# Hybrid encoder step: chunk 1's operands behind the residual, chunk 2 first in the last products, and products without a reader at both ends

## The chip, the cores and the metric

The kernel runs on one core of a Trainium2 chip. The metric is the device time of one execution in microseconds (us). The median of three runs before is 1571.35 us (1571.05 to 1572.93). A profiled execution, recorded apart, gives the span, the busy times and the timeline that the text reads. Its times count from the first instruction of the span.

The engines are named as in the profile: PE (TensorE, matrix products; PEld its weight loads), DVE (VectorE), ACT (ScalarE), POOL (GpSimd) and SP (SyncE, which issues nearly all DMAs here). Each works through its own queue in order and waits for the others on semaphores.

## The reference, cut to what matters

One layer runs over 1152 rows (1024 of a prompt and 128 of eight short streams) with 1024 features. The change touches the end of the first sub-layer and the feed-forward part:

```python
def layer(x, ...):
    h = rmsnorm(x, p['g_pre1'])
    z = h @ p['w_in']
    ...
    x = x + rmsnorm(merged @ p['w_out'], p['g_post1'])
    h2 = rmsnorm(x, p['g_pre2'])
    f, conv_new = conv_ffn(h2, conv_buf, p['w_ffn_up'], p['w_dw'], p['b_dw'], p['w_ffn_down'])
    x = x + rmsnorm(f, p['g_post2'])

def conv_ffn(h, buf, w_ffn_up, w_dw, b_dw, w_ffn_down):
    up = h @ w_ffn_up
    a, g = jnp.split(up, 2, axis=-1)
    ...
    act = jax.nn.gelu(conv) * g
    return act @ w_ffn_down, ext[:, -(CONV_W - 1):]
```

`rmsnorm` divides each row by the root of its mean square and scales by a gain. `w_ffn_up` is 1024 x 5632, `w_ffn_down` 2816 x 1024.

## The kernel before, in words

Activations lie with features on the 128 partitions and rows along the free dimension. The 1152 rows are cut into three **chunks** c = 0, 1, 2 of 384 columns. Every f32 product is made of three products of split operands (`mm3`, lines 102 to 108): each operand has a hi part, written by ACT as a copy, and a lo part, which is the difference and is made on DVE or POOL (`split`, lines 61 to 65). So an operand costs ACT one copy and DVE one subtraction (L63, L64), and a tile of 8 feature blocks costs PE 24 products (L104, L107, L108).

A **row norm** goes through four engines: squares on ACT, sums over partitions as small products with a vector of ones on PE, `rsqrt` (L85 on ACT, L87 a power on POOL), three diagonal tiles on ACT (`row_bcast`, L95), and one f32 product on PE (L97) that spreads the row factors over all partitions into a PSUM bank. DVE then multiplies rows by it.

`start` makes the first products of chunk 0 as soon as the first features of x and the first weights have been loaded and split.

`phase_o` multiplies by `w_out`, chunk after chunk, then adds the residual (`resid`: L1103 scales by the row factors, L1107 adds x, squares L1058 and L1061 on ACT, their sums L1065 on DVE) and norms again (`norm`, L1125). Chunks 0 and 1 enter the up GEMM in Strassen-Winograd form: B11, B21 are the halves of chunk 0, B12, B22 the halves of chunk 1, and T1 to T4 are sums of them; all of these are operands to be split (`op`). While chunk 2's residual and norm are made, PE works on four tiles of the up GEMM for chunk 0 and four for chunk 1 (`plain`: s0 and s1 are the first two blocks of `w_ffn_up`, "a" and "g" its two halves). L1170, L1202 to L1204 make the T sums on DVE. Chunk 2 goes through the up GEMM plainly, from `h2hi` and `h2lo`.

`phase_u` runs the other 20 blocks, `phase_d` the down GEMM: seven products M1 to M7 for chunks 0 and 1 over four groups of features, plain products for chunk 2 into y2. The sums of the parts M make the result rows (L1633 to L1648). The last four feature blocks are added as whole products, `last_down`, in the order of chunks 0, 1, 2; PE holds eight PSUM banks in turn (four `ps`, four `pc`), and DVE adds each bank to its row (L1560). Between these, `final_rms` and `final_rows` norm the chunk before (L1598 scales, L1600 on DVE and L1601 on POOL add x2, SP stores y).

A scheduler orders the instructions of each engine by a simulated timeline; `high_priority`, `issue_after` and `keep_in_program_order` bind it where the code says so.

Of the kernel before, what the change touches and what calls it, by code (L numbers as in the profile page):

```python
# [32 lines left out]
class K:  # L33
# [27 lines left out]
    def split(self, hi, lo, src, eng=None):  # L61
        nc = self.nc
        a = nc.scalar.activation(hi, src, AF.Copy)  # L63
        (eng or nc.vector).tensor_sub(lo, src, hi)  # L64
        return a

# [191 lines left out]
    def start(self, P, pair, done, z):  # L258
        nc = self.nc
        self.hhi, self.hlo = [], []  # L260
        sh = (128, 4, 256)
        I = self.I
        x0 = self.h_load(0, (0,))
        halves = slice(0, 4), slice(4, 8)
        rw = [self.rawtile([128, 8, 128])]
# [765 lines left out]
    def phase_o(self):  # L1031
# [6 lines left out]
        if True:  # L1038
# [50 lines left out]
            def resid(c, rs):  # L1089
# [4 lines left out]
                for f in range(8):  # L1094
# [10 lines left out]
                    if f % 2:  # L1105
                        for k in range(2):
                            pin(V.tensor_add(oT[:, f - 1 + k, :], oT[:, f - 1 + k, :], x[:, k, :]))  # L1107
                    if f % 2:
# [33 lines left out]
            for c in range(3):  # L1142
                ss.append(ssa())
                for f in range(8):
# [7 lines left out]
                    if c:  # L1152
                        if f == 0:
                            rs = sums(ss[c - 1])
                        elif f == 1:
                            with tc.high_priority():
                                ss2 = resid(c - 1, rs)
                        elif f == NF[c]:
                            rs = sums(ss2)
                        elif f == NF[c] + 1:  # L1160
                            with tc.high_priority():
                                norm(c - 1, rs)
                            if c == 1:
                                op("B11", h0[:, lo])
                                op("B21", h0[:, up])
                                V.tensor_sub(h0[:, up], h0[:, up], h0[:, lo])
                            else:
                                op("B12", h1[:, lo])
                                op("B22", h1[:, up])
                                V.tensor_sub(h0[:, lo], h1[:, lo], h0[:, lo])  # L1170
                                op("T1", h0[:, lo])
            wms.close()
# [18 lines left out]
            with tc.high_priority():  # L1191
                ss2 = resid(2, rs)
            plain(s1, "a", 0)
            plain(s1, "g", 0)
# [6 lines left out]
            plain(s1, "g", 1)  # L1201
            V.tensor_sub(h1[:, lo], h1[:, up], h1[:, lo])  # L1202
            V.tensor_sub(h1[:, up], h1[:, up], h0[:, lo])
            V.tensor_sub(h0[:, up], h0[:, up], h1[:, lo])  # L1204
            with tc.issue_after(last.ins):
                op("T3", h1[:, lo])
# [152 lines left out]
    def phase_d(self):  # L1359
# [6 lines left out]
        with ExitStack() as ctx:  # L1366
# [188 lines left out]

            def last_down(last, c, f, acc):

# [8 lines left out]
                nc.scalar.activation(sq, y, AF.Square)  # L1566
                if c == 2 and f > 5:
                    acc.append(sq)
# [14 lines left out]

            def final_rows(c, rs):

# [4 lines left out]
                for f in range(0, 8, 2):  # L1590
                    if c == 1:
                        x2 = self.rawtile([128, 2, 384], "x2r")
# [7 lines left out]
                    order(V.tensor_add(y[0], y[0], x2[:, 0, :]))  # L1600
                    G.tensor_add(y[1], y[1], x2[:, 1, :])  # L1601
                    for k in range(2):
# [22 lines left out]
            for g in range(NW):  # L1625
# [5 lines left out]
                prod(cur, 2)  # L1631
                if last:
                    G.tensor_add(M[2], M[2], M[1])  # L1633
                for f in range(8):
# [3 lines left out]
                for p in (3, 4, 5, 6, 7):  # L1638
                    prod(cur, p)
                    if last and p == 6:  # L1640
                        V.tensor_add(M[6], M[6], M[1])
                        V.tensor_add(M[5], M[5], M[6])
                        G.tensor_add(M[4], M[4], M[6])
                        V.tensor_add(M[3], M[3], M[5])
                    if last and p == 7:
                        for f in range(4):
                            V.tensor_add(M[4][:, f], M[4][:, f], M[7][:, f])
                        G.tensor_add(M[5], M[5], M[7])  # L1648
                    next(nx, None)
# [3 lines left out]
            accs = Mt[3][:, 1].rearrange("p (c k) n -> p c k n", c=2)  # L1653
            acc = [[accs[:, c % 2, 0]] for c in range(3)]
            rows = iter(())
            for c in range(3):
                for f in range(8):
                    last_down(cur, c, f, acc[c])
                    if c:
                        if f == 1:  # L1660
                            rs = final_rms(acc[c - 1])
                        elif f == 3:
                            rows = final_rows(c - 1, rs)
                            next(rows)
                        elif f > 3:
                            next(rows, None)
                if c == 1:
                    for _ in rows:
                        pass
            with tc.issue_after(self.evac.ins):  # L1670
                rs = final_rms(acc[2])
                for _ in rows:
                    pass
            for _ in final_rows(2, rs):
                pass
# [178 lines left out]
```

## Time and profile before

| | |
|---|---|
| median of 3 runs | 1571.35 us |
| profiled execution, its own time | 1571.99 us |
| its span, first to last instruction | 1570.2 us |
| mean granted clock of PE | 0.991 |
| DMA moved | 161.34 MB, 103 GB/s |

The span is 1.8 us shorter than the execution's own time. Busy times are shares of that span. In a timeline row stand the start and the duration in us, engine, line, operation, output and inputs by the program's names, shapes, the count of merged instructions, and in brackets the idle time of the engine before it with what ended it. A duration of a product is longer than the distance to the next product, since products overlap; the pace is read from start to start. The page's row PEclk is the granted clock of PE in tenths.

### The profile page before, as it was taken

How to read it: one execution, taken by the hardware profiler on the slowest of the kernel's cores; microseconds unless marked ns; L12 is line 12 of the kernel's file. 1: busy time of each engine (PE TensorE's matmuls, PEld its weight loads, DVE VectorE, ACT ScalarE, POOL GpSimd, SP SyncE). 2: the span in 40 equal slices, each digit the busy share in tenths (PEclk: the TensorE clock that was granted, in tenths of full speed). 3: DMA queues.
4: the chain of work that ended last, by engine and by line, in shares of the span. 5: the costliest groups of instructions: out<-in, count | busy, mean ns of one | idle time of the engine just before them, and what ended most of it. 6: DMA issues, size and time to landing. Idle time of an engine off the chain costs nothing.

```text
span 1570.2 us, 22880 instructions
## 1 busy us (share of the span) xinstructions
PE 1535.1 (98%) x8988; PEld 1503.1 (96%) x8988; DVE 1018.3 (65%) x1606; ACT 583.3 (37%) x895; POOL 447.9 (29%) x427
## 2 busy tenths in 40 slices
PE   8999999999999999999899999999999999999996
PEld 7999998888999999999899999999999999999996
DVE  8956987656533364547576665665566569788866
ACT  8313444344311251444354333333333343333322
POOL 0000010000111234200215444344344301575446
PEclk9999999999999999999999999999999999999998
DMA  7533334432422234223213212112221234222315
GB/s 269 168 104 103 104 113 164 133 104 80 159 71 72 82 105 148 93 83 117 91 44 116 84 56 85 71 58 82 71 83 57 84 129 137 77 94 90 111 46 171
DMA packets 98028, 161.34 MB, mean 103 GB/s; under 512 B 23168, under 2 KB 68608, under 8 KB 97920
## 3 DMA queue, kind: packets, MB, share of 16 engines
q1 hardware_dynamic: 97488, 159.65, 30.9%
q8 instruction: 70, 1.15, 0.3%
q14 instruction: 38, 0.31, 0.1%
q10 hardware_dynamic: 432, 0.23, 0.1%
HBM read 117.43 MB, written 42.42 MB: 102 GB/s over the span
## 4 chain that ended last, share of the span: by engine, by line
PE 85%; DVE 7%; DMA 3%; issue 2%; ACT 1%; POOL 1%; SPq 0%; POOLq 0%; ACTq 0%; DVEq 0%
PE pc L108 16%; PE pc L107 16%; PE pc L104 16%; PE ps L104 11%; PE ps L107 11%; PE ps L108 11%; DMA Ts<-DG 1%; DMA DG<-gs 1%; PE ps L850 1%; POOL rs_y L87 1%; DVE mg L1125 0%; PE ps L97 0%; PE ps L764 0%; PE ps L816 0%; DVE Xs L599 0%
## 5 line engine op out<-in xcount | busy, mean ns | idle before, releaser
L104 PE MATMUL pc<-hhi,whi 128*128 128x384 f32 x760 | 258.0, 339 | 6.6 <-ACT hhi L127 6.6
L107 PE MATMUL pc<-hlo,whi 128*128 128x384 f32 x760 | 257.2, 338 | 0.1
L108 PE MATMUL pc<-hhi,wlo 128*128 128x384 f32 x760 | 256.7, 338 | 0.3 <-DVE wlo L64 0.3
L63 ACT ACTIVATE whi<-rawt 128x1024 fp32r<-128x1024 f32 (+1 forms) x99 | 103.5, 1047 | 189.0 <-PE pc L107 85.5
L64 DVE TENSOR_TENSOR wlo<-rawt,whi 128x1024 fp32r<-128x1024 f32 (+1 forms) x99 | 122.4, 1238 | 56.3 <-ACT whi L63 56.0
L104 PEld LDWEIGHTS pc<-hhi,whi 128*128 128x128 f32 x760 | 143.5, 189 | 9.1 <-ACT hhi L127 6.6
L107 PEld LDWEIGHTS pc<-hlo,whi 128*128 128x128 f32 x760 | 143.5, 189 | 2.3 <-issue 0.5
L108 PEld LDWEIGHTS pc<-hhi,wlo 128*128 128x128 f32 x760 | 143.4, 189 | 2.3 <-issue 0.7
L201 DVE TENSOR_TENSOR sg<-pc,rb 128x384 f32<-128x384 f32 x95 | 52.4, 554 | 115.5 <-PE pc L108 113.7
L108 PE MATMUL pc<-h2hi,wlo 128*128 128x384 f32 x352 | 118.9, 338 | 0.0
L107 PE MATMUL pc<-h2lo,whi 128*128 128x384 f32 x352 | 118.3, 336 | 0.5 <-DVE h2lo L64 0.5
L104 PE MATMUL pc<-h2hi,whi 128*128 128x384 f32 x352 | 118.3, 336 | 0.0
L63 ACT ACTIVATE S<-S 128x512 fp32r<-128x512 f32 x80 | 50.3, 629 | 149.2 <-PE ps L108 88.9
L64 DVE TENSOR_TENSOR S<-S,S 128x512 fp32r<-128x512 f32 x80 | 66.6, 835 | 49.7 <-ACT S L63 47.7
L925 ACT ACTIVATE sg<-sg,vec 128x384 f32<-128x384 f32 x72 | 44.1, 613 | 139.8 <-DVE sg L201 112.0
L104 PE MATMUL ps<-bT,S 128*128 128x384 f32 x240 | 80.2, 334 | 0.0
L107 PE MATMUL ps<-bT,S 128*128 128x384 f32 x240 | 80.2, 334 | 0.0
L108 PE MATMUL ps<-bT,S 128*128 128x384 f32 x240 | 80.2, 334 | 0.0
L1012 POOL TENSOR_TENSOR mg<-mg,sgl 128x384 f32<-128x384 f32 x24 | 29.1, 1213 | 165.6 <-DVE sgl L1010 162.2
L63 ACT ACTIVATE dhi<-dwr 128x1024 fp32r<-128x1024 f32 x38 | 39.6, 1058 | 83.2 <-PE pc L107 54.6
L87 POOL TENSOR_TENSOR rs_y<-rs_v,mhalf 128x3 f32<-128x3 f32 (+1 forms) x13 | 18.8, 1445 | 174.8 <-ACT rs_v L85 174.7
L107 PEld LDWEIGHTS pc<-h2lo,whi 128*128 128x128 f32 x352 | 66.0, 187 | 0.8 <-DVE h2lo L64 0.8
(446 smaller groups left out, 4277.8 us busy)
## 6 DMA issues: line engine op xcount, KB each, us to landing
rawt<-in_w_up SPq DMA_DIRECT2D x44, 512.0 KB, 3.4
Dact<-t SPq DMA_DIRECT2D x22, 576.0 KB, 3.6
rawt<-in_w_gate SPq DMA_DIRECT2D x24, 512.0 KB, 3.5
dwr<-in_w_down SPq DMA_DIRECT2D x22, 512.0 KB, 3.5
Dsg<-sg SPq DMA_DIRECT2D x45, 192.0 KB, 1.9
sgl<-Dsg SPq DMA_DIRECT2D x45, 192.0 KB, 2.4
dBr<-Dact SPq DMA_DIRECT2D x8, 768.0 KB, 5.1
xT<-in_xT SPq DMA_DIRECT2D x12, 384.0 KB, 7.2
```

The costliest lines, as they stand in the source:

```text
L63: a = nc.scalar.activation(hi, src, AF.Copy)
L64: (eng or nc.vector).tensor_sub(lo, src, hi)
L87: nc.gpsimd.tensor_tensor(y, v, self.mhalf[:, 0:n], op=OP.pow)
L104: i = nc.tensor.matmul(out, whi, xhi, start=start, stop=False)
L107: nc.tensor.matmul(out, whi, xlo, start=False, stop=False)
L108: nc.tensor.matmul(out, wlo, xhi, start=False, stop=stop)
L201: self.nc.vector.tensor_mul(sg, b, self.rb[:, c, :])
L850: nc.tensor.matmul(o, va[:, m, 2 * hp + e, :], pT[:, m, :], start=m == 0, stop=m == 1)
L925: self.nc.scalar.activation(sg, sg, AF.Sigmoid, bias=self.vec[:, V_BGATE + m:V_BGATE + m + 1])
L1012: nc.gpsimd.tensor_add(m, m, sp)
```

## The change

Four edits:

1. In `start`, a memset of the row-factor tile and eight f32 products of it with the ones tile are put ahead of the first product. Nothing reads their result.
2. In `phase_o`, the copies of B12 and B22 are issued after the diagonal tiles of chunk 2's residual, and the subtraction and copy for T1 after the residual's last add (`resid_last`). `split` returns both its instructions, so that the last two subtractions for T2 and T4 can be issued after the last lo part of h2.
3. In `phase_d`, the last products run over chunks 2, 0, 1. The sums of parts are written between chunk 2's last products, one of POOL's goes to DVE, and the rows of a normed chunk start one product tile earlier. The last add of the last chunk goes from POOL to DVE.
4. Ahead of the last row broadcast twelve products of the last operands are put into a free bank. Nothing reads their result.

```diff
@@ split
         a = nc.scalar.activation(hi, src, AF.Copy)
-        (eng or nc.vector).tensor_sub(lo, src, hi)
-        return a
+        return a, (eng or nc.vector).tensor_sub(lo, src, hi)
@@ start
         x0 = self.h_load(0, (0,))
+
+        rb = self.rb[:, 0]
+        nc.vector.memset(rb, 0.0)
+        b = self.sm()[:, 0:384]
+        for _ in range(8):
+            self.tc.keep_in_program_order(nc.tensor.matmul(b, self.ones, rb, start=True, stop=True))
@@ phase_o, resid
-                            pin(V.tensor_add(oT[:, f - 1 + k, :], oT[:, f - 1 + k, :], x[:, k, :]))
+                            self.resid_last = V.tensor_add(oT[:, f - 1 + k, :], oT[:, f - 1 + k, :], x[:, k, :])
+                            pin(self.resid_last)
@@ phase_o, after norm of chunk 1
-                            else:
-                                op("B12", h1[:, lo])
-                                op("B22", h1[:, up])
-                                V.tensor_sub(h0[:, lo], h1[:, lo], h0[:, lo])
-                                op("T1", h0[:, lo])
@@ phase_o, after plain(s0, "g", 0) and resid(2, rs)
+            with tc.issue_after(self.diag.ins):
+                op("B12", h1[:, lo])
+                op("B22", h1[:, up])
+            with tc.issue_after(self.resid_last.ins):
+                V.tensor_sub(h0[:, lo], h1[:, lo], h0[:, lo])
+                op("T1", h0[:, lo])
+                V.tensor_sub(h1[:, lo], h1[:, up], h1[:, lo])
@@ phase_o, end
-            V.tensor_sub(h1[:, lo], h1[:, up], h1[:, lo])
-            V.tensor_sub(h1[:, up], h1[:, up], h0[:, lo])
-            V.tensor_sub(h0[:, up], h0[:, up], h1[:, lo])
-            with tc.issue_after(last.ins):
+            with tc.issue_after(last[1].ins):
+                V.tensor_sub(h1[:, up], h1[:, up], h0[:, lo])
+                V.tensor_sub(h0[:, up], h0[:, up], h1[:, lo])
+            with tc.issue_after(last[0].ins):
@@ phase_d, last_down and final_rows
-                if c == 2 and f > 5:
+                if end and f > 5:
...
-                    if c == 1:
+                    if i == 2:
...
-                    G.tensor_add(y[1], y[1], x2[:, 1, :])
+                    (V if (i, f) == (3, 6) else G).tensor_add(y[1], y[1], x2[:, 1, :])
@@ phase_d, last group
-                if last:
-                    G.tensor_add(M[2], M[2], M[1])
...
-                    if last and p == 6:
-                        V.tensor_add(M[6], M[6], M[1])
-                        V.tensor_add(M[5], M[5], M[6])
-                        G.tensor_add(M[4], M[4], M[6])
-                        V.tensor_add(M[3], M[3], M[5])
-                    if last and p == 7:
-                        for f in range(4):
-                            V.tensor_add(M[4][:, f], M[4][:, f], M[7][:, f])
-                        G.tensor_add(M[5], M[5], M[7])
@@ phase_d, last products
+            sums = {(0, 0): ((G, 2, 1), (V, 6, 1)), (0, 1): ((V, 4, 6),), (0, 3): ((V, 4, 7),), (0, 4): ((V, 5, 6),),
+                    (0, 6): ((V, 3, 5),), (0, 7): ((G, 5, 7),)}
+            order = (2, 0, 1)
+            for i, c in enumerate(order):
                 for f in range(8):
-                    last_down(cur, c, f, acc[c])
-                    if c:
+                    last_down(cur, c, f, acc[i], i == 2)
+                    for e, p, q in sums.get((i, f), ()):
+                        e.tensor_add(M[p], M[p], M[q])
+                    if i:
                         if f == 1:
-                            rs = final_rms(acc[c - 1])
+                            rs = final_rms(acc[i - 1])
                         elif f == 3:
-                            rows = final_rows(c - 1, rs)
+                            rows = final_rows(order[i - 1], rs, i)
                             next(rows)
-                        elif f > 3:
-                            next(rows, None)
-                if c == 1:
-                    for _ in rows:
-                        pass
+                        if 2 < f < (7 if i == 1 else 6):
+                            next(rows)
...
+            b = bank()
+            s = cur[0]
+            for _ in range(12):
+                tc.keep_in_program_order(nc.tensor.matmul(b, s.wh[:, 0:128], s.hi[:, 0:384], start=True, stop=True))
-            for _ in final_rows(2, rs):
+            for _ in final_rows(order[2], rs, 3):
                 pass
```

The scheduler turns this into new places on the engines. Line numbers of the changed kernel differ by up to eight from those before: what was L85 is L84, L95 is L94, L1186 is L1187. First the queue of ACT in `phase_o`, between chunk 1's norm and chunk 2's residual. bB are the hi parts of B12 and B22, bT that of T1, ax and g the evacuations of `plain`, rs_v and diag the first and third step of the row factors. Before:

```order
L63 ACTIVATE bB_7270<-mg_4094 128x1536
L1186 ACTIVATE ax<-pc 128x384
L63 ACTIVATE bB_7273<-mg_4094 128x1536
L85 ACTIVATE rs_v<-ps 128x3
L63 ACTIVATE bT_7277<-mg_4093 128x1536
L95 ACTIVATE diag<-ident,rs_y 128x128 x3
L1186 ACTIVATE g<-pc 128x384
```

And in the changed kernel, to the second row factor:

```order
L1187 ACTIVATE ax<-pc 128x384
L84 ACTIVATE rs_v<-ps 128x3
L94 ACTIVATE diag<-ident,rs_y 128x128 x3
L63 ACTIVATE bB_7416<-mg_4104 128x1536
L63 ACTIVATE bB_7419<-mg_4104 128x1536
L1187 ACTIVATE g<-pc 128x384
...
L1187 ACTIVATE g<-pc 128x384
L63 ACTIVATE bT_7423<-mg_4103 128x1536
L84 ACTIVATE rs_v<-ps 128x3
L94 ACTIVATE diag<-ident,rs_y 128x128 x3
```

The three wide copies moved from ahead of the first diag to behind it, and T1's copy now stands ahead of the second rs_v. On DVE at the same place (lo parts L64; mg_4095 before and mg_4105 in the change is chunk 2) stood before:

```order
L64 TENSOR_TENSOR bB_7270<-mg_4094,bB_7270 128x1536
L64 TENSOR_TENSOR bB_7273<-mg_4094,bB_7273 128x1536
L64 TENSOR_TENSOR bT_7277<-mg_4093,bT_7277 128x1536
L1202 TENSOR_TENSOR mg_4094<-mg_4094 128x1536
L1103 SCALAR_TENSOR_TENSOR mg_4095<-mg_4095,vec,ps 128x384 x2
L1203 TENSOR_TENSOR mg_4094<-mg_4094,mg_4093 128x1536
L1204 TENSOR_TENSOR mg_4093<-mg_4093,mg_4094 128x1536
L1107 TENSOR_TENSOR mg_4095<-mg_4095,x 128x384 x2
```

and stands now:

```order
L64 TENSOR_TENSOR bB_7416<-mg_4104,bB_7416 128x1536
L1108 SCALAR_TENSOR_TENSOR mg_4105<-mg_4105,vec,ps 128x384 x2
L64 TENSOR_TENSOR bB_7419<-mg_4104,bB_7419 128x1536
L1112 TENSOR_TENSOR mg_4105<-mg_4105,x 128x384 x2
...
L1112 TENSOR_TENSOR mg_4105<-mg_4105,x 128x384 x2
L1198 TENSOR_TENSOR mg_4103<-mg_4104,mg_4103 128x1536
L1200 TENSOR_TENSOR mg_4104<-mg_4104 128x1536
L64 TENSOR_TENSOR bT_7423<-mg_4103,bT_7423 128x1536
```

Four wide instructions of 128x1536 went from between the residual's steps to behind its last add.

On DVE around the last lo copy of `phase_d` (act is the operand of the last feature block; M_11785 holds M5 and M6, M_11784 M3 and M4, M_11783 M1 and M2) stood before:

```order
L64 TENSOR_TENSOR act<-dar,act 128x1152
L1642 TENSOR_TENSOR M_11785<-M_11785 128x1536
L1488 TENSOR_TENSOR M_11786<-M_11786,ps 128x384
L1488 TENSOR_TENSOR M_11786<-M_11786,pc 128x384
L1560 TENSOR_TENSOR M_11783<-M_11783,ps 128x384
L1647 TENSOR_TENSOR M_11784<-M_11784,M_11786 128x384 x2
L1644 TENSOR_TENSOR M_11784<-M_11784,M_11785 128x1536
L1647 TENSOR_TENSOR M_11784<-M_11784,M_11786 128x384 x2
```

and stands now (numbers of tiles are ten higher; L1568 is the evacuation that was L1560):

```order
L64 TENSOR_TENSOR act<-dar,act 128x1152
L1661 TENSOR_TENSOR M_11794<-M_11794,M_11795 128x1536
L1661 TENSOR_TENSOR M_11795<-M_11795 128x1536
L1496 TENSOR_TENSOR M_11796<-M_11796,ps 128x384
L1496 TENSOR_TENSOR M_11796<-M_11796,pc 128x384
L1568 TENSOR_TENSOR y_11797<-y_11797,ps 128x384
L1568 TENSOR_TENSOR y_11797<-y_11797,pc 128x384
L1661 TENSOR_TENSOR M_11794<-M_11794,M_11795 128x1536
L1661 TENSOR_TENSOR M_11794<-M_11794,M_11796 128x1536
```

The sum of M4 and M6, which was POOL's (L1643), is now on DVE behind the lo copy, and the evacuations go to chunk 2's y first.

More of the change, by code (lines that the diff above doesn't have):

```diff
@@ L1554, in row, with last_down @@
                 return M[((2, 4), (3, 5))[c][f // 4]][:, f % 4]
-            def last_down(last, c, f, acc):
+            def last_down(last, c, f, acc, end):
                 b = whole_mm(last, c, f, True)
@@ L1582, in final_rms, with final_rows @@
                     return self.rsqrt(P, ss, 3)
-            def final_rows(c, rs):
+            def final_rows(c, rs, i):
                 with tc.high_priority():
@@ L1653, in phase_d @@
             accs = Mt[3][:, 1].rearrange("p (c k) n -> p c k n", c=2)
-            acc = [[accs[:, c % 2, 0]] for c in range(3)]
+            acc = [[accs[:, i % 2, 0]] for i in range(3)]
             rows = iter(())
-            for c in range(3):
+            sums = {(0, 0): ((G, 2, 1), (V, 6, 1)), (0, 1): ((V, 4, 6),), (0, 3): ((V, 4, 7),), (0, 4): ((V, 5, 6),),
+                    (0, 6): ((V, 3, 5),), (0, 7): ((G, 5, 7),)}
+            order = (2, 0, 1)
+            for i, c in enumerate(order):
                 for f in range(8):
-                    last_down(cur, c, f, acc[c])
-                    if c:
+                    last_down(cur, c, f, acc[i], i == 2)
+                    for e, p, q in sums.get((i, f), ()):
+                        e.tensor_add(M[p], M[p], M[q])
+                    if i:
                         if f == 1:
-                            rs = final_rms(acc[c - 1])
+                            rs = final_rms(acc[i - 1])
                         elif f == 3:
-                            rows = final_rows(c - 1, rs)
+                            rows = final_rows(order[i - 1], rs, i)
                             next(rows)
-                        elif f > 3:
-                            next(rows, None)
-                if c == 1:
-                    for _ in rows:
-                        pass
+                        if 2 < f < (7 if i == 1 else 6):
+                            next(rows)
             with tc.issue_after(self.evac.ins):
```

## The prediction

> **What bounds the kernel now.** I read the page's busy line and clock row first, then the waits of TensorE, then stretches of the timeline around each long wait.
>
> ```profile
> PE 1535.1 (98%) x8988; PEld 1503.1 (96%) x8988; DVE 1018.3 (65%) x1606; ACT 583.3 (37%) x895; POOL 447.9 (29%) x427
> ...
> PEclk9999999999999999999999999999999999999998
> ```
>
> TensorE (PE) is busy for 1535.1 us of 1570.2, so only the 35 us between can be won, besides products that run at a lower clock. The 40 slices are too coarse for the clock: only the last shows less than full. Next come the waits of PE, in us in total, times, longest:
>
> ```profile
> PE ps L97 <- ACT diag L95: 5.0, 2, 4.8
> ...
> PE ps L107 <- DVE act L64: 2.0, 1, 2.0
> ...
> PE ps L1073 <- DVE ssa L1065: 1.3, 2, 0.9
> PE ps L1073 <- ACT sq L1061: 1.2, 1, 1.2
> ```
>
> The timeline puts the 4.8 us and most of L1073 into the end of `phase_o`, and the 2.0 us at the start of the last products of the down GEMM. The windows there (us; busy time of PE, PEld, DVE, ACT, POOL with counts; granted clock) show that a wait costs twice:
>
> ```profile
> 772.50:777.00 4.50, 4.44 (x12) 3.84 (x13) 2.75 (x4) 0.38 (x2) 0.00 (x0) 0.52 0.00 0
> 1500.00:1510.00 10.00, 10.00 (x50) 10.00 (x49) 10.00 (x11) 0.52 (x1) 3.77 (x1) 0.83 0.00 0
> ```
>
> After the wait the clock is 0.52 in the first and 0.83 in the second. Full speed is this pair of rows, 27 products apart:
>
> ```profile
> 1505.37 0.33 PE L104 MATMUL ps<-act,dhi 128*128 128x384 f32 x1
> ...
> 1510.06 0.34 PE L104 MATMUL pc<-act,dhi 128*128 128x384 f32 x1
> ```
>
> 4.69 us by 27 is 0.174 us a product; a tile of 24 takes 4.17 us.
>
> The Trainium skill, "TensorE: Matmul & The Clock Gate", Part 1, lets the clock fall to half after at least one idle window of about 3.4 us, on windows that run free. By that the gap of 2.0 us at 1497 would not lower the clock and part B below would give 1.3 instead of 2.8; the row with 0.83 speaks against it.
>
> **Part A: operands of chunk 1 behind the residual.** Before, chunk 1's operand copies stand ahead of chunk 2's row factors:
>
> ```profile
> 760.37 1.49 ACT L63 ACTIVATE bB<-mg 128x1536 fp32r<-128x1536 f32 x1 [1.82 <-DVE mg L1125]
> ...
> 764.02 3.42 DVE L64 TENSOR_TENSOR bB<-mg,bB 128x1536 fp32r<-128x1536 f32 x2
> ...
> 769.02 1.76 DVE L1202 TENSOR_TENSOR mg<-mg 128x1536 f32<-128x1536 f32 x1
> ...
> 764.37 7.11 POOL L87 TENSOR_TENSOR rs_y<-rs_v,mhalf 128x3 f32<-128x3 f32 x1 [6.89 <-ACT rs_v L85]
> ...
> 771.52 0.98 ACT L95 ACTIVATE diag<-ident,rs_y 128x128 f32<-128x128 f32 x3 [5.89 <-POOL rs_y L87]
> ...
> 767.44 0.34 PE L108 MATMUL pc<-bB,wlo 128*128 128x384 f32 x1
> 772.56 1.65 PE L97 MATMUL ps<-diag,ones 128*128 128x384 f32 x2 [4.79 <-ACT diag L95]
> ...
> 796.94 0.85 POOL L87 TENSOR_TENSOR rs_y<-rs_v,mhalf 128x3 f32<-128x3 f32 x1 [25.45 <-ACT rs_v L85]
> ...
> 802.30 0.81 PE L97 MATMUL ps<-diag,ones 128*128 128x384 f32 x2
> ```
>
> The power of three columns on POOL (L87) takes 0.85 us at 796.94, but 7.11 us at 764.37, where DVE runs wide two-input instructions without a gap until 770.8. It ends 0.7 us after them. So the wait of 4.79 us is POOL held up by DVE. The Trainium skill, "SBUF — State Buffer", section "Who interferes with whom", has the later instruction of the two blocked until the one that runs is finished. By that L87 would be late by one copy, about 1.7 us, and removing the block would win some 3 us less; here it outlasted all of them, so the measured row decides.
>
> In the changed order ACT has rs_v and diag ahead of the copies bB, and DVE has nothing between the rows of chunk 1 and the first bB. Rs_v can start at the end of the sums, about 763.4, L87 takes 0.85, diag 0.98: 765.5, while PE reaches L97 at 767.6. The cover is 2 us. The copies then end on ACT at 768.4 and on DVE (1.71 each, with two residual steps between) at 768.7 and 771.4; the first product that reads them starts at 767.6 + 0.8 + 2 x 4.17 = 776.8, a cover of 5 us.
>
> What is late next is the residual itself:
>
> ```profile
> 774.25 1.14 DVE L1103 SCALAR_TENSOR_TENSOR mg<-mg,vec,ps 128x384 f32<-128x384 f32 x2 [3.47 <-PE ps L97]
> ...
> 778.64 1.02 DVE L1107 TENSOR_TENSOR mg<-mg,x 128x384 f32<-128x384 f32 x2
> ...
> 785.20 0.56 DVE L1065 TENSOR_TENSOR ssa<-ssa,sq 128x384 f32<-128x384 f32 x1 [5.53 <-ACT sq L1061]
> ```
>
> Four times 1.14 + 1.02, one copy (1.71), five adds of 0.5 and three waits for squares of about 0.6 that ACT makes between PE's evacuations: from 768.6 to about 783.6, the last square at 784.2. PE asks for the sums at 776.8 + 2 x 4.17 = 785.1; cover 0.9 us. The x loads have the same places on SP and start earlier. Then comes the new order's own risk: on ACT, T1's copy (1.49) stands ahead of rs_v, and it waits for DVE's subtraction (1.75). So rs_v starts at 787.2, L87 is held by DVE's lo copy to 788.9 and ends at 789.7, diag at 790.8. PE is there at 785.1 + 1.1 (nine small products, from the six in 0.72 below) + 4.17 = 790.4: a new wait of 0.5 us. L97 at 790.9 instead of 802.30 is **11.4 us less**. It contains the waits of 4.8 and 2.1 and the half clock behind both. Bounds: 11.9 without the new wait; 6 if the squares wait on ACT as in the 5.53 us row.
>
> Two subtractions (2 x 1.75) now follow the h2lo copies, so DVE is 3.5 us later with the operands S and T of the next stage:
>
> ```profile
> 821.88 2.49 DVE L64 TENSOR_TENSOR S<-S,S 128x512 fp32r<-128x512 f32 x4
> ...
> 833.06 0.33 PE L104 MATMUL ps<-bT,S 128*128 128x384 f32 x1
> ```
>
> The last S is ready at 824.4, the first product that reads one starts at 833.06: 8.7 us of cover, 5.2 left. I take 0; without cover it would cost up to 3.5.
>
> **Part B: sums of parts among the last products, chunk 2 first.**
>
> ```profile
> 1494.91 3.50 POOL L1643 TENSOR_TENSOR M<-M,M 128x1536 f32<-128x1536 f32 x1 [21.02 <-DVE M L1641]
> ...
> 1488.90 1.35 DVE L64 TENSOR_TENSOR act<-dar,act 128x1152 fp32r<-128x1152 f32 x1
> ...
> 1496.80 2.83 DVE L64 TENSOR_TENSOR act<-dar,act 128x1152 fp32r<-128x1152 f32 x1 [1.03 <-ACT act L63]
> ...
> 1499.68 0.44 PE L107 MATMUL ps<-act,dhi 128*128 128x384 f32 x1 [1.98 <-DVE act L64]
> ...
> 1505.21 4.34 DVE L1647 TENSOR_TENSOR M<-M,M 128x384 f32<-128x384 f32 x2
> ```
>
> The last lo copy takes 2.83 us beside POOL's sum L1643, 1.35 alone. In the change that sum is DVE's and stands behind the copy. So the copy ends at 1498.15, and PE waits 0.5 to 0.65 us instead of 1.98: **1.3 us**. A gap this short (0.5 us at other places) leaves the clock as it is, so the half clock of 1500 to 1510 goes: 0.17 x 10 us, less a little: **1.5 us**. The sums move onto DVE among the evacuations of chunk 2, about 4 x 1.75 us in 16.7 us; PE is eight PSUM banks ahead, so I cost them at nothing.
>
> **Part C: the end.**
>
> ```profile
> 1553.92 0.54 DVE L1560 TENSOR_TENSOR y<-y,pc 128x384 f32<-128x384 f32 x1
> ...
> 1552.66 0.72 PE L1577 MATMUL ps<-ones,M 128*128 128x1 f32 x6
> ...
> 1555.59 1.24 POOL L1601 TENSOR_TENSOR M<-M,x2r 128x384 f32<-128x384 f32 x1 [0.74 <-DVE M L1598]
> 1556.86 0.86 POOL L87 TENSOR_TENSOR rs_y<-rs_v,mhalf 128x3 f32<-128x3 f32 x1
> ...
> 1558.79 1.65 PE L97 MATMUL pc<-diag,ones 128*128 128x384 f32 x2 [2.22 <-ACT diag L95]
> ...
> 1543.66 0.81 PE L97 MATMUL pc<-diag,ones 128*128 128x384 f32 x2
> ...
> 1566.26 1.24 POOL L1601 TENSOR_TENSOR y<-y,x2r 128x384 f32<-128x384 f32 x1 [0.27 <-DVE y L1598]
> ```
>
> The last products end at about 1552.8, but their evacuation starts at 1553.92, behind chunk 1's rows on DVE. With the rows one place earlier and none between the last two evacuations it follows PE: 1.0 us, of which I keep **0.8**, as the square sums of the second chunk may come 0.2 late. On SP the stores of chunk 2 come first now; no PE work waits for a store. L87 stays behind POOL's row add (to 1556.83), which moves with the evacuation. The twelve products without reader (12 x 0.174 = 2.1 us) fit between the last sums and L97, and L97 takes 0.81 instead of 1.65 if the clock holds: **0.8**. The last add on DVE ends 0.4 us before POOL's 1567.5 (an add there is 0.5): **0.4**.
>
> **Part D: the start.**
>
> ```profile
> 6.58 0.69 PE L104 MATMUL pc<-hhi,whi 128*128 128x384 f32 x1 [6.58 <-ACT hhi L127]
> ...
> 11.98 0.45 PE L104 MATMUL pc<-hhi,whi 128*128 128x384 f32 x1
> ...
> 25.75 0.95 ACT L608 ACTIVATE Xs<-h 64x32 f32<-64x32 f32 x4
> ...
> 29.33 0.91 PE L97 MATMUL ps<-diag,ones 128*128 128x384 f32 x2 [0.23 <-ACT diag L95]
> ```
>
> Until 12 us a product takes about 0.32. The eight new f32 products (1.65 each at half clock, 0.81 at full, as bounds from L97) stand ahead of the first product in PE's queue and run from about 1.2 us, when their two memsets are done. If the clock comes after 2 to 5 us (it came 5.4 us after 6.58), they end between 7.5 and 9.5, up to 3 us after the first operand. The first tile makes that up at full clock and ends near 12.0, with DVE's last hlo, not at 13.7, but at 29.33 PE waits for diag already, whose rs_v stands behind ACT's L608 copies to 26.7: only **0.2 us** remain of 1.7. Bounds: -0.5 to +0.8.
>
> **Sum.** 11.4 + 1.3 + 1.5 + 0.8 + 0.8 + 0.4 + 0.2 = 16.4 us. The profiled execution took 1571.99 us (its span 1570.2), so 1555.6; the median of the runs is 0.6 lower, which gives **1555.0 us**.
>
> **Rivals.**
> (1) The residual becomes the bound: squares queue on ACT behind evacuations that wait for PE, as in the 5.53 us row, or T1's copy holds rs_v back further. Part A gives 6: 1560.4 us. For it: the cover of 0.9 us; against: PE no longer runs late, so those evacuations come early.
> (2) The power on POOL is still held up, so that the order doesn't do what it says: then only part of B to D and the 1 to 2 us of waits at L1073: about 1565. Against: no wide DVE instruction stands there in the new order.
> (3) Slower: DVE's four sums meet POOL's sums as in the 4.34 us row, 4.3 times their time of 1.01. Four sums of 1.75 at that factor are 30 us in 16.7 us of products; PE stalls on PSUM banks and its clock halves. The whole gain is lost from a factor of about 5 (35 us less 16.7), and then it is some 1574 us. Against: POOL has two such sums, and the contention lasts no longer than they do, 3.5 us each.
> (4) The end runs at half clock: 12 x 0.32 = 3.8 us push L97 back by 0.6 and it stays at 1.65: 1556.5, inside the forecast's own range.
>
> **Chances.** Forecast 0.70 (1552.5 to 1559, with (4)), (1) 0.20, (2) 0.06, (3) 0.04. The range 1552.5 to 1562 leaves out (2), (3) and the edges. Faster or slower counts from 0.2%, about 3 us, which is what a measurement of this kernel can tell from no change; (2) still is faster. Faster 0.94, same 0.03, slower 0.03.
>
> **What would show it.** In the profile of after: L87 of the residual at 0.85 us and no wait at the L97 behind it; L97 of chunk 2's second norm 11 us earlier; no stretch of half clock near 775, 798 and 1500; the lo copy at 1.35; L97 at the end at 0.81. Wrong it would be by a new wait of over 1 us before the sums L1073 or in the chunk 2 products, with a half clock behind it.

## The result and the profile after

| | before | after |
|---|---|---|
| median of 4 runs | 1571.75 us (1571.05 to 1572.93) | 1557.34 us (1553.49 to 1557.83) |
| ratio of the times | | 0.9902, 95% interval 0.9885 to 0.9919 |
| profiled execution, its own time | 1571.99 us | 1553.49 us |
| its span | 1570.2 us | 1551.6 us |

The changed kernel is 14.4 us faster in the median, where 16.4 had been summed; its profiled execution, the fastest of the four, is 18.5 us faster than the one of before. Both lie inside the range. Line numbers are up to 10 away from before: L84, L86, L94 and L96 are the row factors, the power, the diagonal tiles and the row broadcast.

The page of after, busy line and clock row: PE works as long as before (1535 us), and only the idle went.

```profile
PE 1535.3 (99%) x9016; PEld 1502.2 (97%) x9016; DVE 1018.7 (66%) x1606; ACT 583.5 (38%) x895; POOL 442.1 (28%) x425
...
PEclk9999999999999999999999999999999999999998
```

The waits of PE in after (in total, times, longest): the 4.8 us behind the diagonal tiles and the 2.0 us for the last lo part are gone, and of the 2.5 us at the sums 0.4 are left. What is left is 1.4 us or less each; the longest is that of the eight new products at the start.

```profile
PE ps L268 <- DVE pr L395: 1.4, 1, 1.4
PE ps L96 <- ACT diag L94: 1.3, 1, 1.3
PE ps L635 <- DVE Xs L604: 1.0, 1, 1.0
...
PE pc L106 <- DVE h2lo L64: 0.5, 1, 0.5
PE ps L1078 <- DVE ssa L1070: 0.4, 1, 0.4
```

The windows of after at the places of before (busy time of PE, PEld, DVE, ACT, POOL with counts; then the granted clock): 1.00 where it was 0.52 and 0.83. The last row is the end of the kernel, where the clock fell all the same.

```profile
765.50:770.00 4.50, 4.50 (x26) 4.24 (x25) 4.50 (x6) 1.32 (x2) 0.00 (x0) 1.00 0.00 0
...
1485.00:1495.00 10.00, 10.00 (x59) 10.00 (x58) 9.73 (x11) 2.15 (x5) 5.19 (x2) 1.00 0.13 49
...
1538.72:1542.13 3.41, 3.38 (x9) 2.02 (x7) 0.00 (x0) 0.99 (x3) 0.65 (x1) 0.50 0.26 99
```

The timeline of after, the rows that answer to those of before: the residual's power takes 0.85 us instead of 7.11, the second norm's broadcast runs at 789.07 instead of 802.30, the last lo copy takes 1.36 instead of 2.83, and PE's first last product comes without a wait. At the end the power still stands behind POOL's row add, and the broadcast takes 1.56, not 0.81.

```profile
761.82 0.85 POOL L86 TENSOR_TENSOR rs_y<-rs_v,mhalf 128x3 f32<-128x3 f32 x1 [6.37 <-ACT rs_v L84]
...
765.58 0.81 PE L96 MATMUL ps<-diag,ones 128*128 128x384 f32 x2
...
785.28 2.17 POOL L86 TENSOR_TENSOR rs_y<-rs_v,mhalf 128x3 f32<-128x3 f32 x1 [22.61 <-ACT rs_v L84]
...
789.07 0.81 PE L96 MATMUL ps<-diag,ones 128*128 128x384 f32 x2
...
1482.63 1.36 DVE L64 TENSOR_TENSOR act<-dar,act 128x1152 fp32r<-128x1152 f32 x1 [0.53 <-ACT act L63]
1484.09 0.33 PE L103 MATMUL ps<-act,dhi 128*128 128x384 f32 x1
...
1537.30 1.26 POOL L1609 TENSOR_TENSOR M<-M,x2r 128x384 f32<-128x384 f32 x1 [1.60 <-DVE M L1606]
1538.52 0.85 POOL L86 TENSOR_TENSOR rs_y<-rs_v,mhalf 128x3 f32<-128x3 f32 x1
...
1540.54 1.56 PE L96 MATMUL pc<-diag,ones 128*128 128x384 f32 x2
```

**Where the 18.6 us of span came from.** I matched PE's products of both traces one by one and read by how much after is ahead:

| up to | after is ahead by | part |
|---|---|---|
| first row broadcast, 29 us | -0.55 | start |
| 235 us | 1.77 | start and middle |
| end of `phase_o` | 13.21 | A: 11.44 |
| first last products, then 5 us on | 15.41, 17.08 | B: 2.20 wait, 1.67 clock |
| end of the span | 18.6 | C: 1.5 |

A and C come close to the prediction. B is larger, and 1.8 us appear at 233 us, where nothing was changed. The row at 29 us says little: in the twelve profiles of this study that broadcast starts anywhere from 29.33 to 30.81 us.

### The profile page after: what moved, and what is told of

Its sections match the earlier page's. It is cut to its first block, busy times and chain, and to the rows that moved or that the text cites. A ratio compares the mean times of both kernels' runs of the same rounds, so it can differ in the third digit from the quotient of the medians.

```text
span 1551.6 us, 22930 instructions
## 1 busy us (share of the span) xinstructions
PE 1535.3 (99%) x9016; PEld 1502.2 (97%) x9016; DVE 1018.7 (66%) x1606; ACT 583.5 (38%) x895; POOL 442.1 (28%) x425
## 3 DMA queue, kind: packets, MB, share of 16 engines
q8 instruction: 70, 1.15, 0.3%
## 4 chain that ended last, share of the span: by engine, by line
PE 88%; DVE 6%; DMA 2%; ACT 2%; issue 1%; SPq 0%; POOL 0%; DVEq 0%; ACTq 0%; POOLq 0%
PE pc L107 16%; PE pc L103 16%; PE pc L106 16%; PE ps L103 11%; PE ps L106 11%; PE ps L107 11%; DMA Ts<-DG 1%; PE ps L855 1%; DMA DG<-gs 1%; ACT hhi L126 1%; DVE mg L1131 1%; PE ps L1078 0%; PE ps L769 0%; PE ps L821 0%; DVE Xs L604 0%
## 5 line engine op out<-in xcount | busy, mean ns | idle before, releaser
L64 DVE TENSOR_TENSOR wlo<-rawt,whi 128x1024 fp32r<-128x1024 f32 (+1 forms) x99 | 122.5, 1239 | 54.6 <-ACT whi L63 54.2
L64 DVE TENSOR_TENSOR S<-S,S 128x512 fp32r<-128x512 f32 x80 | 68.7, 861 | 46.2 <-ACT S L63 44.2
L107 PEld LDWEIGHTS pc<-h2hi,wlo 128*128 128x128 f32 x352 | 66.1, 188 | 0.0
```

The source lines that it names most:

```text
L64: return a, (eng or nc.vector).tensor_sub(lo, src, hi)
L107: nc.tensor.matmul(out, wlo, xhi, start=False, stop=stop)
```

## The experiments

Each variant differs from the changed kernel as its diff says, and is compared with kernels measured together with it. There were three such series after the first result: **again**, **no_start**, **old_o** and **old_last** (before: 1571.12 us in the median); **one_col**, **no_end**, **full_end** and **old_o_copy** (1571.01); **t1_early** and **tuned_end** (1570.24).

### The same again, and each edit undone

**again**: no edit.

> The changed kernel once more. Its four times so far lie in two groups, 1553.5 us (the profiled one) and 1557.2 to 1557.8; before lay within 1.9 us. Theory S: the groups come from the start, where the clock can come up in different places under the eight products without reader; then a profile of the upper group has its first full clock some 3.4 us later than 6.13 us and everything behind it is late by 2 to 4 us. Theory M: one of the short waits in the middle (0.96 us at 232, 0.52 at 794, 0.83 at 1296, 0.65 at 1339) is sometimes followed by 3.4 us of half clock, worth 1.7 us each. Theory E: the end, where the clock fell at 1538.72 in the profile so far. I expect two groups again, and that no stretch before 1500 us shows a half clock except the start.

Measured: 1555.68 us (1554.43 to 1556.33). No two groups this time, so I hold the eight runs of the changed kernel for one spread, 1553.5 to 1557.8. Its profile again has no half clock before 1500 us but the start. It does not say where the spread comes from; the profiles show places where runs differ.

It shows a difference from after: at the last products of the down GEMM PE waits again.

```profile
PE ps L106 <- DVE act L64: 0.8, 1, 0.8
```

The lo copy takes 1.36 us as in after. But in every profile ACT's copy ahead of it starts 0.08 us after the load of that operand has landed, and the load takes 4.7 us from issue to landing in after and 5.9 in **again**. **no_start**, **old_o**, **one_col** and **tuned_end**, which have the third edit too, wait 0.7 to 1.0 us there, with loads of 5.6 to 6.3 us. So it is luck that after has no wait there: five of the ten profiles with this edit have none.

**no_start**:

```diff
-        rb = self.rb[:, 0]
-        nc.vector.memset(rb, 0.0)
-        b = self.sm()[:, 0:384]
-        for _ in range(8):
-            self.tc.keep_in_program_order(nc.tensor.matmul(b, self.ones, rb, start=True, stop=True))
```

> The changed kernel without the memset and the eight products at its start; all else in the same order. By my term D this is slower by 0.2 us only. Theory S: the two groups are gone, all times within 2 us, and the median is at or below that of the changed kernel. Theory M or E: two groups as before. Rival to term D: the profile so far stood 1.8 us ahead of before at 233 us; if the products gave that, this kernel is 1.8 us slower.

Measured: 1558.73 us (1556.44 to 1559.23), 3.05 slower than **again**; the two sets of runs don't overlap. Term D (0.2) is too small, and theory S is wrong: without the products the spread is as wide. At 30 us this kernel is only 0.3 us behind after, near what the prediction had; at 236 us it is 3.6 us behind. The timeline of no_start shows what is late in between, the store of gs on SP (DG) and PE's wait for Xs, which hangs on it by a load, ACT, POOL and DVE:

```profile
149.54 1.28 SPq L542 DMA_DIRECT2D DG<-gs  x1
...
181.51 1.89 SPq L542 DMA_DIRECT2D DG<-gs  x1
...
236.46 0.48 PE L629 MATMUL ps<-Xs,ar 128*128 128x144 f32 x2 [2.17 <-DVE Xs L598]
```

The same rows of after:

```profile
149.28 0.37 SPq L548 DMA_DIRECT2D DG<-gs  x1
...
180.52 0.61 SPq L548 DMA_DIRECT2D DG<-gs  x1
...
232.84 0.48 PE L635 MATMUL ps<-Xs,ar 128*128 128x144 f32 x2 [0.96 <-DVE Xs L604]
```

The DMA view of no_start from 148.7 to 150.5 us, by queue (packets, MB, share of 16 engines), has one packet that after, from 149.2 to 151.0, has not: 16 KB of instructions, on one of 16 engines for 1.73 us.

```profile
q8 instruction: 1, 0.02, 6.0%
```

That is theory F of the run **one_col** below. The three stores at 150, 182 and 217 us take 0.91, 1.28 and 1.07 us longer in no_start than in after, 3.26 us together, and from 30 to 236 us PE falls 3.30 us further behind. Before's three take 2.81 us longer than after's, and before falls 2.32 us behind. The windows of no_start also show a half clock at 345 us, in products that no edit touches:

```profile
341.85:345.26 3.41, 3.41 (x29) 3.10 (x28) 3.04 (x2) 0.99 (x2) 0.00 (x0) 1.00 0.31 90
345.26:348.68 3.42, 3.42 (x13) 3.42 (x13) 1.34 (x2) 0.00 (x0) 0.00 (x0) 0.50 0.84 234
```

So the 3.05 us of the runs can hold some of the clock as well. The 3.30 us of the trace lie ahead of it and do not.

**old_o**: the operands of chunk 1 and T1 ahead of the residual and the three subtractions for T2 and T4 at the end of `phase_o`, as before.

```diff
+                            else:
+                                op("B12", h1[:, lo])
+                                op("B22", h1[:, up])
+                                V.tensor_sub(h0[:, lo], h1[:, lo], h0[:, lo])
+                                op("T1", h0[:, lo])
...
-            with tc.issue_after(self.diag.ins):
...
-            with tc.issue_after(self.resid_last.ins):
...
```

> The changed kernel with its second edit undone: operands of chunk 1 and T1 ahead of chunk 2's residual again, the other three edits kept. My theory: 11.4 us slower, with the power on POOL at 7 us beside DVE's unbroken two-input instructions, a wait of about 4.8 us before the residual's row broadcast, and half clock behind it and behind the second norm's sums. Rival: part of that gain came from elsewhere (start and middle), then it is 8 us slower or less.

Measured: 1566.02 us (1564.89 to 1566.34), 10.3 slower than **again**; in the traces 10.9 between the places before and behind `phase_o`. The timeline of old_o, POOL and DVE: the power ends at 770.10, 0.7 us behind DVE's train, which has no gap (each instruction starts before the end of the one ahead).

```profile
762.99 7.11 POOL L86 TENSOR_TENSOR rs_y<-rs_v,mhalf 128x3 f32<-128x3 f32 x1 [6.89 <-ACT rs_v L84]
...
762.64 3.42 DVE L64 TENSOR_TENSOR bB<-mg,bB 128x1536 fp32r<-128x1536 f32 x2
765.98 1.76 DVE L64 TENSOR_TENSOR bT<-mg,bT 128x1536 fp32r<-128x1536 f32 x1
767.64 1.76 DVE L1208 TENSOR_TENSOR mg<-mg 128x1536 f32<-128x1536 f32 x1
```

**old_last**: the third edit undone.

```diff
-            order = (2, 0, 1)
-            for i, c in enumerate(order):
+            for c in range(3):
...
-                    (V if (i, f) == (3, 6) else G).tensor_add(y[1], y[1], x2[:, 1, :])
+                    G.tensor_add(y[1], y[1], x2[:, 1, :])
```

> The changed kernel with its third edit undone: last products in the order of chunks 0, 1, 2, sums of parts before them, rows a tile later, last add on POOL; the other edits kept. My sum: 2.8 us (wait 1.3, half clock 1.5) + 0.8 + 0.4 = 4.0 us slower; by the trace of after, which showed no wait at all there (2.0 us gone, not 1.3), 4.7 us. Rival: the wait at the first last product hangs on the copy of the last operands alone and comes back without the half clock: 2.5 us slower.

Measured: 1558.77 us (1556.84 to 1559.13), 3.1 slower than **again**. PE's waits in old_last have the wait back:

```profile
PE ps L106 <- DVE act L64: 1.4, 1, 1.4
```

No half clock follows it in this profile: the rival holds here, and my 4.0 to 4.7 took for certain a clock that fell behind before's wait of 1.98 us and not behind this one of 1.4. The rest is mostly the end: from the last product to the end of the span 17.8 us instead of 16.3.

The three undone edits together cost 10.3 + 3.1 + 3.05 = 16.5 us; before stood 15.4 us behind **again** in the same series. So within the spread of the runs the parts add up.

### What holds what

**one_col**: the eight products at the start with one column each.

```diff
-            self.tc.keep_in_program_order(nc.tensor.matmul(b, self.ones, rb, start=True, stop=True))
+            self.tc.keep_in_program_order(nc.tensor.matmul(b[:, 0:1], self.ones, rb[:, 0:1], start=True, stop=True))
```

> The changed kernel with its eight products at the start cut to one column each: the same count and order of instructions on every engine, but too little work to bring the clock up. Theory F (instruction fetch): the kernel without the eight products was 3 us slower because 16 KB instruction fetches for PE at 148.7, 181.5 and 216.8 us run beside the stores of gs and make the loads behind them late; with the products these fetches come 1.5 us earlier relative to the stores. Then this kernel has the stores' issues at 0.4 to 0.7 us as in the changed kernel, PE's wait at 233 us near 1 us, and a time within 1 us of the changed kernel (1555.7). Theory C (clock): the 3 us come from the early clock; then it stands near the kernel without the products (1558.7).

Measured: 1556.17 us (1553.71 to 1557.12) in the second series, whose before is 0.1 us from the first's. The clock comes at 12.27 us, as in before, not at 6.13; yet at 233 us PE stands where it does in after (232.89 against 232.84). Theory F holds, theory C falls. The stores in one_col:

```profile
148.24 0.37 SPq L548 DMA_DIRECT2D DG<-gs  x1
...
180.03 1.21 SPq L548 DMA_DIRECT2D DG<-gs  x1
```

One expectation missed: the second store took 1.21, not 0.4 to 0.7, since a fetch from 179.88 to 180.85 runs beside it here. That fits F. Over the 12 profiles of this study with these three stores each (a fourth, at 132 us, meets no fetch in any), by the single packets in the traces: the issue takes 0.37 us where no fetch runs (20 of 36), and otherwise 0.37 us more than the fetch has left, within 0.07 us. In before and no_start all three stores meet a fetch, in every kernel with the eight products only the second.

**old_o_copy**: old_o, with one-input copies on DVE in place of the subtractions; the lo parts of B12, B22 and T1 and the T1 sum aren't computed.

```diff
-                self.split(t[:, 0], t[:, 1], src, eng)
+                if name in ("B12", "B22", "T1"):
+                    nc.scalar.activation(t[:, 0], src, AF.Copy)
+                    V.tensor_copy(t[:, 1], src)
+                else:
+                    self.split(t[:, 0], t[:, 1], src, eng)
...
```

> The kernel with the second edit undone (operands of chunk 1 ahead of the residual again), but with the lo parts of B12, B22 and T1 and the T1 sum as copies: DVE's train of wide instructions there has one input each and no two-input instruction; the subtraction is left out. Theory T: the power on POOL was held for 7.1 us by DVE's two-input instructions; here it takes about 0.85 us and the wait before the residual's broadcast is under 1 us. Rival W: any train of wide DVE instructions holds POOL up; then the power again ends about 0.7 us behind the last of them, and takes over 3 us.

Measured: 1556.06 us, a single run; 3.91 us for the power, with 1.6 us as the longest wait before a broadcast. The timeline of old_o_copy, POOL and DVE:

```profile
762.40 3.91 POOL L86 TENSOR_TENSOR rs_y<-rs_v,mhalf 128x3 f32<-128x3 f32 x1 [6.89 <-ACT rs_v L84]
...
762.12 0.95 DVE L1142 CAST bB<-mg 128x1536 fp32r<-128x1536 f32 x1
762.99 0.95 DVE L1142 CAST bT<-mg 128x1536 fp32r<-128x1536 f32 x1
763.86 1.75 DVE L1212 TENSOR_TENSOR mg<-mg 128x1536 f32<-128x1536 f32 x1
765.71 1.76 DVE L1213 TENSOR_TENSOR mg<-mg,mg 128x1536 f32<-128x1536 f32 x1
```

The power would have been done at 763.25 if copies let it pass, before the first two-input instruction: theory T falls. It ends at 766.31, 0.7 us behind the end of L1212 at 765.61. There DVE stood still for 0.1 us, and the next wide instruction no longer held it. So what holds POOL is a train of wide DVE instructions without a gap, copies of this kind (0.95 us for 128x1536) too, and the first gap ends it. In before, old_o, old_o_copy and at 787 us in after alike the power ends 0.70 us behind the instruction that held it last. Whether narrow copies hold it as well was not tried.

**t1_early**: T1's subtraction and operand behind the diagonal tiles, not behind the residual.

```diff
+                V.tensor_sub(h0[:, lo], h1[:, lo], h0[:, lo])
+                op("T1", h0[:, lo])
             with tc.issue_after(self.resid_last.ins):
-                V.tensor_sub(h0[:, lo], h1[:, lo], h0[:, lo])
-                op("T1", h0[:, lo])
                 V.tensor_sub(h1[:, lo], h1[:, up], h1[:, lo])
```

> The changed kernel with T1's subtraction, copy and lo part behind the diagonal tiles like B12 and B22, not behind the residual's last add. PE's order is the same. My rival 1 (the residual becomes the bound) would show here: DVE has 3.5 us more to do ahead of the last squares, which in the changed kernel come 0.4 us before PE asks for the sums. DVE's waits for squares in the residual (1.0 + 0.9 + 0.2 us) take up to 2.1 of it; so PE waits 1.0 to 3.1 us before the sums, and the kernel is that much slower, 1.7 more where a window falls to half clock. Other theory: only freeing the power of DVE's train matters, T1's place doesn't; then the time is within 0.5 us of the changed kernel and no wait stands before the sums.

Measured: 1555.13 us (1553.42 to 1555.79), as fast as the changed kernel. My expectation missed. PE's wait for the sums of a residual is one, the 0.4 us that after has too (chunk 0's, at 722 us):

```profile
PE ps L1078 <- DVE ssa L1070: 0.4, 1, 0.4
```

T1's subtraction ran at 762.45, where DVE waited for ACT's copy anyway. The power takes 0.96 us:

```profile
763.95 0.96 POOL L86 TENSOR_TENSOR rs_y<-rs_v,mhalf 128x3 f32<-128x3 f32 x1 [6.37 <-ACT rs_v L84]
```

Rival 1 of the prediction had less ground than it was given, and the place of T1 isn't what edit 2 lives on: it is that no train of DVE stands beside the power.

### The end

**no_end**: the twelve products taken out.

```diff
-            for _ in range(12):
-                tc.keep_in_program_order(nc.tensor.matmul(b, s.wh[:, 0:128], s.hi[:, 0:384], start=True, stop=True))
```

> The changed kernel without the twelve products at its end. Theory N: they did nothing, since the clock had already fallen by the 2.1 us of idle PE between the last product (1535.4) and the first of them (1537.5), and the row broadcast took 1.56 us, not 0.81; then from the first sums (1535.42 in the profile of after) to the end of the span this kernel takes the same 16.1 us within 0.3. My term: they are worth 0.8 us; then it takes 16.9. The time is within 1 us of the changed kernel either way, since the windows of the clock fall differently in each run.

Measured: 1555.54 us (1554.13 to 1556.81); from the first sums to the end of the span 16.1 us, as in after: theory N holds for this pair. But in no_start and old_o (and t1_early), which keep the twelve products, the clock held to the broadcast, and there the end came 15.6 us behind the last product, against 16.3 in after, again, one_col, old_o_copy and no_end. The 16.3 come about in two ways. Without the products, and in after, the broadcast itself runs at half clock:

```profile
1543.14 1.65 PE L96 MATMUL pc<-diag,ones 128*128 128x384 f32 x2 [2.76 <-ACT diag L94]
```

In again the clock fell earlier: the twelve products ran at half clock and ended late, and the broadcast, at 0.81 us, began 0.9 us after the diagonal tiles were ready at 1541.56 (in one_col 0.8 us).

```profile
1538.70 3.89 PE L1678 MATMUL ps<-act,dhi 128*128 128x384 f32 x12
1542.43 0.81 PE L96 MATMUL pc<-diag,ones 128*128 128x384 f32 x2
```

In no_start they ran at full clock and the broadcast waited for the tiles only:

```profile
1543.63 2.36 PE L1672 MATMUL ps<-act,dhi 128*128 128x384 f32 x12
1546.55 0.91 PE L96 MATMUL pc<-diag,ones 128*128 128x384 f32 x2 [0.56 <-ACT diag L94]
```

So the products are worth 0.7 us in some runs and nothing in others.

**full_end** and **tuned_end**: products without reader ahead of the last sums too, and the row add ahead of the last power on DVE. `idle(b, n)` puts n such products into a bank; the diff is full_end's, tuned_end has 2 and 12.

```diff
-                    (V if (i, f) == (3, 6) else G).tensor_add(y[1], y[1], x2[:, 1, :])
+                    (V if i > 1 and f == 6 else G).tensor_add(y[1], y[1], x2[:, 1, :])
...
+            idle(bank(), 5)
             with tc.issue_after(self.evac.ins):
                 rs = final_rms(acc[2])
...
+            idle(b, 16)
```

> The changed kernel with five products without reader ahead of the last sums, sixteen instead of twelve behind them, and the last row add of the middle chunk on DVE, so that the power on POOL isn't behind it. I expect no idle of PE above 0.5 us between the last product and the row broadcast, the broadcast at 0.81 us, the power 0.6 us earlier, and 14.8 us instead of 16.1 from the first sums to the end of the span; about 1554.4 us in the median. Rival: the five products delay the last sums, or the clock falls all the same; then 16 us or more.

Measured: 1555.00 us (1554.45 to 1555.73), and 16.15 us from the last product to the end: nearly the 16.3 of after, though the clock held. Counted from the first sums, as in the expectation, it is 15.1 instead of 14.8, but the five products put these sums back by 0.9 us, as the rival had it, and the power came no earlier. The timeline of full_end: the five products hold the sums up, and the sixteen run past 1541.8, when the diagonal tiles are ready.

```profile
1536.69 1.04 PE L1672 MATMUL ps<-act,dhi 128*128 128x384 f32 x5
1537.57 0.72 PE L1585 MATMUL ps<-ones,M 128*128 128x1 f32 x6
1538.15 1.48 PE L1585 MATMUL ps<-ones,sq 128*128 128x1 f32 x12
1539.49 3.06 PE L1672 MATMUL pc<-act,dhi 128*128 128x384 f32 x16
1542.39 0.81 PE L96 MATMUL pc<-diag,ones 128*128 128x384 f32 x2
```

> As the kernel with the full end, but two products ahead of the last sums instead of five and twelve instead of sixteen behind them, the row add still on DVE. Five products held the last sums up by 0.7 us and sixteen ran 0.5 us into the row broadcast's place. From the last product to the end of the span the changed kernel takes 16.3 us with the clock at half at the broadcast and the same without its twelve products; 15.6 where the clock held. I expect the power at 2.7 us behind the last product (3.3 before), the broadcast at 4.6 and the end at 15.0, with the clock at full whatever the run, and 1554.5 us in the median. Rival: two products leave more than 2.1 us of one window idle, the clock falls in some runs, and then the end is at 15.7.

Measured: 1554.29 us (1553.09 to 1555.36), ratio to before 0.9900 (0.9886 to 0.9914); 15.2 us from the last product to the end, near the 15.0 expected and 1.1 less than in after, with the broadcast at full clock. This is the lowest median of the study. Against the changed kernel (1556.06 over its eight runs) the ranges overlap, so its gain is shown by the trace, not by the times.

## Why the prediction was right, step by step

- **A (11.4 us)**: 11.44 in the profile, 10.3 in the runs of old_o. The mechanism held: power 0.85 us, no wait at the broadcast, no half clock. The new wait of 0.5 us did not come: the power was held up to 2.17 us by the lo copy, as foreseen, but the diagonal tiles were ready at 788.5, not 790.8, and PE came at 789.07.
- **B (1.3 + 1.5)**: the lo copy came to 1.36 as foreseen. In after the wait went to nothing, so 2.2 instead of 1.3; in five of the other profiles with this edit 0.7 to 1.0 us of it stayed, where 0.5 to 0.65 had been forecast. The copy is the cause that the prediction named; what it left out is that the landing of the last load sets when the copy starts. The clock's 1.5 came to 1.67 in the profile; it was lost behind before's wait of 1.98 us and not behind old_last's 1.4.
- **C (0.8 + 0.8 + 0.4)**: the power comes 1.1 us earlier behind the last product (3.28 instead of 4.37), the last add on DVE gives its 0.4, and the broadcast's 0.8 is missing. Rival 4 had a broadcast put back by 0.6 and run at half clock as well; the runs show mostly one or the other, for about 0.7 us.
- **D (0.2)** was mis-sized. On its own path, to 30 us, the products gain 0.3 us at most (after against no_start), and the profiles differ there by more than that. What it lacked is a second effect of eight more products in PE's stream, 2.3 us from 29 to 235 us between before and after and 3.05 in the runs of no_start: they move the instruction fetches off two of the three stores of gs.
- **Rivals**: 2 left no trace (no such wait). Of 3 little is seen: the sums on DVE, five and not four, take 1.75 us but for one of 2.58 beside POOL's, and PE does not stall on them. 1 was tried by t1_early and did not show.
- **The median** (14.4 instead of the profile's 18.5): the sum was made for the profiled execution, and the runs spread by 4.3 us, which no term foresaw. The clock falls by windows that lie differently in each run; 1.7 us at 342 to 350 us hit 5 of the 10 profiles taken after the first, and 0.7 at the end 5 of the 8 profiles that have the twelve products and nothing more there. Of the three unprofiled runs above 1557 no trace exists, so that this is their cause was not shown. That the sum of 16.4 lies between the two is in part luck: the gain at 233 us that it lacked stands against the broadcast's 0.8 that did not come and this spread.

## What to carry to other kernels

A small operation on POOL that the critical path needs must not stand beside a train of wide DVE instructions: put it ahead of the train, or leave the train a gap. Products without reader keep the clock only if they fill the idle inside a window, and they must be counted against the wait, since each one too many delays the next real product. A change of a few instructions on PE can move times far away from it by moving instruction fetches, so an edit's worth is read at its own place in the trace first and in the total second.

## What the runs showed of the hardware that was not expected

**The clock's windows.** All stretches of half clock between products are multiples of 3.41 us, and the grid lies differently against the start in each run (full clock from 12.22, 6.13, 10.76, 4.71 us). I worked out which share of each window PE streamed columns: 384 columns of a split product take 0.32 us at half clock, its pace there, so 0.16 at full, and an f32 product twice that (0.64 apart at the start of after). In 12 profiles all 27 windows up to 0.35 at full clock were followed by half clock, and none from 0.38 up was (windows taken 0.1 us before the clock's change). Before's wait of 1.98 us gave 0.32 and cost the clock; old_last's 1.4 us gave 0.47 and didn't. The stretch at 342 us, 28 products of 32 columns, lay almost whole in one window of no_start, which came to 0.34, and was divided in after between two, of 0.5 and 0.66. The Trainium skill, "TensorE: Matmul & The Clock Gate", Part 1, has free-running windows of about 3.4 us and half clock after an idle one: the windows agree, but a window a third full is idle enough. The bounds are fitted to these 12 profiles and were tried on no others.

**Instruction fetches.** A 16 KB fetch for PE holds up a DMA issue on SP until it ends, by up to 1.5 us here. (That the fetches are PE's I take from their amount: in after the queue moves 1.15 MB, about 64 bytes for each of PE's 18032 products and weight loads.) The Trainium skill, "Runtime: NRT & Kernel Launch", section "Instruction fetch mechanics", has the fetch in 16 KiB blocks and its cost mostly hidden; the size agrees, and the cost was about 3 us in a chain that waits for three stores.
